# A transformer block pair in float32 on one core: one-bank PSUM tiles for the projections, and combinations recorded ahead of splits

## Chip, cores and metric

The kernel runs on 1 core of a Trainium2 chip. The metric is the device time of one execution in microseconds (us). Before the change three runs gave 1897.74, 1902.15 and 1903.02 us; the median is 1902.15.

## What is computed

Two blocks over 512 tokens of width 2048, all in float32. The first puts 16 learned tokens ahead (528 rows), normalises, projects to queries, keys, values and gates of two attention kinds (8 heads with 2 key/value heads and axial rope; 8 heads of differential attention with a distance bias), gates the results and projects back. The second has stick-breaking attention and a gated linear recurrence. Cut to the part that matters here:

```
hn = rmsnorm(h, pre_norm_g)                      # h: 528 x 2048
proj = einsum('bld,dc->blc', hn, w_in)           # the input projection
qa, ka, va, ga, qb, kb, vb, gb = split(proj)     # ga, gb: gates; qb, kb, vb: differential attention
ya = gqa_axial_mixer(qa, ka, va, ...) * silu(ga)
yb = diff_attn_mixer(qb, kb, vb, ...) * silu(gb)
y  = concatenate([ya, yb]) @ w_out
h  = h + rmsnorm(y, post_norm_g)                 # then the second block on 512 rows
```

## The kernel before

Every float32 operand is split into a high and a low half (`split`, L162: ScalarE casts the high half, L163, and VectorE subtracts it from the source, L164), and a product is three matmul passes over the halves. In the traces L163 and L164 therefore stand for all splits (of weights into wsp, of attention weights into pt, and so on), and L196 for all matmuls, L199 for all transposes.

The work is recorded by a main generator (`main_work`, L1152) and side generators (normalisation, rope, attention heads, the sums of x). `run` (L221) picks the next step by a clock that counts the matmuls' nominal times; a step waits for keys that others post with a delay (`post`, `when`). TensorE's order is fixed by this recording (`_queue`, L187). The order on VectorE, ScalarE and SP is decided afterwards by the recording layer's scheduler, which moves independent instructions past each other. That layer makes an instruction wait for earlier users of the same tile of PSUM.

The order of the main work: keys KA and values VA in channel-major form, queries QA in token-major form (`tm`, L482), the second value (`value(1)`), then 20 pairs of 128-column blocks by a scheme with seven products in place of eight (`seven`, L423), then the output projection O1 and the second block.

In `seven`, TensorE writes four accumulators r[0] to r[3] of one PSUM bank each. A full product is 18 matmuls (6 tiles of 128 rows, three passes); a `rest` adds the 4 remaining tiles, 12 matmuls. The order for a pair is: product 1 into bank 0, product 4 into bank 2, product 5 and rest 6 into bank 0, product 3 into bank 1, rest 6 into bank 3, product 2 into bank 0, product 7 into bank 1, rest 8 into banks 2 and 1, product 9 into bank 3. Between them VectorE combines: L459 reads bank 1 and L460 bank 2 after product 3; L465 and L466 read bank 0 after product 2. Three evacuations end the pair's outputs: `evac_a1` reads bank 0 after rest 6 (L1217 for gates, L1254 for queries and keys, L1280 for values), `evac_b` reads banks 1 and 2 after the rests of 8 (L1222 and L1223 for gates), `evac_a2` reads bank 3 after product 9 (L1230, L1263). p1s keeps product 1 (a ScalarE copy, L450).

The banks come from the pool psj: two tiles of two banks each (L118, L128). Banks 0 and 1 are the halves of one tile, banks 2 and 3 those of the other (L1197).

`produce(p, i)` (L351) splits the weights of product i of pair p and issues the loads and adding transfers that their slots allow. `side_x` (L622) builds the sums and differences of the two halves of x: for six steps j it loads two tiles of x, scales them on ScalarE (L629), combines them on VectorE (L630 to L633) and splits them into x23 and x1s; a last step splits a fourth combination into big once the second value has read that part (key "x2k1"). It begins at 95,000 ns of the recording clock. The first pair waits for all of it (L1196). The tiles of x come from a ring of six (`et`) that attention uses too.

Of the kernel before, what the change touches and what calls it, by code (L numbers as in the profile page):

```python
# [9 lines left out]
F32 = mybir.dt.float32  # L10
# [101 lines left out]
def hybrid_two_block_kernel(ctx: ExitStack, tc: tile.TileContext, wp, wq, wc, xT, xtok, par, lvec, cst, rg, pg, lruw, out):  # L112
# [43 lines left out]
    def halves(ap):  # L156
        return ap.rearrange("p (a b) -> p a b", a=2)
# [60 lines left out]
    def when(*keys):  # L218
        return keys
# [183 lines left out]
    def fm_two(units, ps, lag):  # L403

        w = [None, None]
        for i in range(KT + lag):
            for u, kt in ((0, i), (1, i - lag)):
                if 0 <= kt < KT:
                    if kt % 8 == 0:
                        w[u] = take(units[u], kt // 8, AHEAD - 1)  # L410
                    for pi, (ws, xs) in enumerate(PASSES):
                        for c in range(2):
                            mm(ps[u][:, c, :HL], w[u][:, ws, (kt % 8) * P : (kt % 8 + 1) * P],
                               big[:, xs, kt, c * HL : (c + 1) * HL], kt == 0 and pi == 0, kt == KT - 1 and pi == 2)
                        yield
            if i == KT - 1:
                act.copy(halves(kvraw[0]), ps[0][:, :, :HL])
                post(("kv", 0), 1000)

    def fm_all(unit, ps, after_kt=None):  # L420
        return fm(unit, [(ps[:, 0, :HL], (0, HL)), (ps[:, 1, :HL], (HL, L))], after_kt)

    def seven(p, r, c0a, c0b, evac_a1, evac_b, evac_a2, after=None):  # L423

# [35 lines left out]
        dve.tensor_tensor(us[:], r[2][:, :HL], wv[:], ALU.add)  # L460
# [5 lines left out]
        dve.tensor_tensor(ts[:], r[0][:, :HL], us[:], ALU.add)  # L466
# [12 lines left out]
    def fm_real(unit, ps, x0):  # L479
        return fm(unit, [(ps[:, 0, :], (x0, x0 + NTOK))])  # L480
# [139 lines left out]
    gins = [0]  # L620

    def side_x():  # L622
        ready[("start", 9)] = 95000.0
        yield when(("start", 9), ("kr", 0), ("kr", 1))
        for j in range(KS):
            a, b = et(), et()
            for t, kt in ((a, j), (b, KS + j)):
                nc.sync.dma_start(t, xT[kt])
                act.mul(t, t, g1[:, kt : kt + 1])  # L629
            dve.tensor_tensor(b[:, HL:], a[:, HL:], b[:, HL:], ALU.subtract)  # L630
# [12 lines left out]
    def rope(x, rn, n, c, s, t1, u):  # L643

# [505 lines left out]


    def main_work():  # L1152
        ps = [pjt(), pjt()]
        yield from fm_two((("KA", 0), ("KA", 1)), ps, 3)
        act.copy(halves(kvraw[1]), ps[1][:, :, :HL])
        post(("kv", 1), 1000)
        def value(i, after_kt=None):
            ps = pjt()
            yield from fm_all(("VA", i), ps, after_kt)
            if i:  # L1160
                kvraw[3] = et()
            act.copy(halves(kvraw[2 + i]), ps[:, :, :HL])
            post(("kv", 2 + i), 1000)

        yield from value(0)
# [183 lines left out]
        for hf in range(2):  # L1349
            yield when(("x2", hf))  # L1350
            hc = slice(hf * 256, (hf + 1) * 256)
            for b4 in range(2):
                ps = pjt()
                aps = []
                for i in range(4):
                    ap = ps[:, i // 2, (i % 2) * 256 : (i % 2) * 256 + 256]
                    yield from fm(("XL", 4 * b4 + i), [(ap, (hf * 256, (hf + 1) * 256))])
                    aps.append(ap)
                yield when(("r2", hf))
                for i in range(4):  # L1360
                    b = 4 * b4 + i
                    dve.tensor_tensor(ybuf[:, b, hc], aps[i], rb2[:, hc], ALU.mult)
                    if hf:
                        post(("xl", b))
        for b in range(8):
            ps = pjt()
            yield from fm_real(("GL", b), ps, 0)
            silu2(ps[:, 0, :], rb2, ybuf[:, 8 + b, :])
            post(("gl", b))
        for h in range(8):  # L1370
            ps = pjt()
            yield from fm_real(("GS", h), ps, 0)
            yield when(("xlused", h))
            ins = silu2(ps[:, 0, :], rb2, ybuf[:, h, :])
        with tc.issue_after(ins):
            lnload[1] = act.preload_act_table_set("natural_log_exp_and_others").ins

# [193 lines left out]
```

## Time and profile before

| | |
|---|---|
| median of three runs | 1902.15 us |
| profiled execution | 1903.71 us, span 1901.9 us |
| mean granted TensorE clock | 0.967 |
| busy: TensorE, weight loads, VectorE, ScalarE, GpSimd | 92%, 81%, 60%, 47%, 7% of the span |
| matmuls and transposes | 10288 |
| moved by DMA | 231.72 MB, mean 122 GB/s |
| largest group | 512-column matmuls into pj, 740.0 us |

A row of the busy table gives a stretch, its length, and for each engine its busy time and instruction count; overlapping instructions of one engine count once. A row of the waits names the engine that waited, the tile it wrote and its line, then the engine, tile and line of the instruction that ended the wait, the total in us, the number of waits and the longest. In a timeline row stand the start, the duration, the engine, line, operation, tiles, shape, count, and in brackets the idle time before it with what ended it. A releaser is inferred from semaphore events, so where several conditions were awaited, it is the one that came last.

### The profile page before, as it was taken

How to read it: one execution, taken by the hardware profiler on the slowest of the kernel's cores; microseconds unless marked ns; L12 is line 12 of the kernel's file. 1: busy time of each engine (PE TensorE's matmuls, PEld its weight loads, DVE VectorE, ACT ScalarE, POOL GpSimd, SP SyncE). 2: the span in 40 equal slices, each digit the busy share in tenths (PEclk: the TensorE clock that was granted, in tenths of full speed). 3: DMA queues.
4: the chain of work that ended last, by engine and by line, in shares of the span. 5: the costliest groups of instructions: out<-in, count | busy, mean ns of one | idle time of the engine just before them, and what ended most of it. 6: DMA issues, size and time to landing. Idle time of an engine off the chain costs nothing.

```text
span 1901.9 us, 26572 instructions
## 1 busy us (share of the span) xinstructions
PE 1740.8 (92%) x10288; PEld 1543.1 (81%) x10288; DVE 1139.2 (60%) x1947; ACT 902.5 (47%) x1485; POOL 136.6 (7%) x145
## 2 busy tenths in 40 slices
PE   8997887788887879787998999999999999999998
PEld 8787877788887778787877899988888888888887
DVE  4675666656566668766654676884322375566533
ACT  6354444454444446546643554774222366365411
POOL 0011011100001111110000000010000000000000
PEclk9999989899999899989998999999999999999999
DMA  8335544444544334444334676523232322342223
GB/s 301 116 126 131 158 97 98 110 111 112 138 105 101 88 93 109 97 95 122 128 109 162 220 256 189 158 86 100 89 100 89 100 69 76 100 155 78 89 79 132
DMA packets 82670, 231.72 MB, mean 122 GB/s; under 512 B 9312, under 2 KB 15072, under 8 KB 80864
## 3 DMA queue, kind: packets, MB, share of 16 engines
q1 hardware_dynamic: 73904, 206.43, 33.7%
q0 software_dynamic: 8640, 23.60, 7.9%
q8 instruction: 81, 1.33, 0.3%
q14 instruction: 45, 0.37, 0.1%
HBM read 212.17 MB, written 17.83 MB: 121 GB/s over the span
## 4 chain that ended last, share of the span: by engine, by line
PE 52%; DVE 1%; issue 0%; ACT 0%; DMA 0%; DVEq 0%; ACTq 0%; SPq 0%
PE pj L196 47%; PE pmt L196 1%; PE pss L196 1%; PE bank L196 1%; PE ptt L199 1%; PE pmt L199 0%; PE pss L199 0%; DMA yd<-xmisc 0%; DMA e<-yd 0%; DVE big L164 0%; ACT wsp L163 0%; DVE wsp L164 0%; DVE e L164 0%; DVE e L898 0%; ACT e L901 0%
## 5 line engine op out<-in xcount | busy, mean ns | idle before, releaser
L196 PE MATMUL pj<-wsp,big 128*128 128x512 f32 x3072 | 740.0, 398 | 13.6 <-ACT big L163 8.7
L196 PE MATMUL pj<-big,wsp 128*128 128x264 f32 (+3 forms) x4320 | 662.3, 312 | 86.6 <-DVE xmisc L466 37.1
L196 PEld LDWEIGHTS pj<-big,wsp 128*128 128x128 f32 x4320 | 603.4, 196 | 132.6 <-DVE xmisc L460 35.1
L196 PEld LDWEIGHTS pj<-wsp,big 128*128 128x128 f32 x3072 | 573.1, 189 | 143.0 <-ACT big L163 9.3
L164 DVE TENSOR_TENSOR wsp<-wraw,wsp 128x1024 fp32r<-128x1024 f32 (+3 forms) x399 | 426.4, 1070 | 408.3 <-ACT wsp L163 400.6
L163 ACT CAST wsp<-wraw 128x1024 fp32r<-128x1024 f32 (+3 forms) x399 | 367.9, 924 | 554.0 <-PE pj L196 467.4
L196 PE MATMUL pj<-x,wsp 128*128 128x264 f32 x720 | 112.8, 308 | 40.8 <-DVE e L1217 15.5
L196 PEld LDWEIGHTS pj<-x,wsp 128*128 128x128 f32 x720 | 102.6, 208 | 44.6 <-issue 31.1
L349 POOL DMA_DIRECT2D wraw<-in_wq x60 | 52.8, 880 | 531.0 <-DVE wsp L164 224.2
L164 DVE TENSOR_TENSOR pt<-ptt,pt 128x512 fp32r<-128x512 f32 (+2 forms) x96 | 59.6, 621 | 42.7 <-ACT pt L163 41.8
L163 ACT CAST pt<-ptt 128x512 fp32r<-128x512 f32 (+2 forms) x96 | 50.3, 524 | 67.5 <-PE ptt L199 67.1
L196 PE MATMUL pss<-kk,qq 128*128 128x264 f32 x448 | 75.8, 299 | 3.2 <-DVE sm L898 3.2
L901 ACT ACTIVATE e<-e,sm 128x528 f32<-128x528 f32 x64 | 47.2, 738 | 62.5 <-DVE sm L898 61.9
L196 PE MATMUL pmt<-pt,vv 128*128 128x256 f32 (+1 forms) x528 | 70.2, 281 | 2.9 <-DVE ptail L702 2.9
L196 PEld LDWEIGHTS pmt<-pt,vv 128*128 128x128 f32 x528 | 68.1, 191 | 5.1 <-issue 3.4
L196 PEld LDWEIGHTS pss<-kk,qq 128*128 128x128 f32 x448 | 65.6, 200 | 5.4 <-DVE sm L898 3.7
L898 DVE CUSTOM_DVE_ANT_0 e<-pss,ar 128x528 f32<-128x528 f32 x64 | 45.0, 704 | 25.5 <-PE pss L196 25.3
L199 PE MATMUL ptt<-ident,e 128*128 128x128 f32 x336 | 53.8, 278 | 0.0
L196 PE MATMUL pj<-x1s,wsp 128*128 128x264 f32 x360 | 53.7, 297 | 0.0
L196 PEld LDWEIGHTS pj<-x1s,wsp 128*128 128x128 f32 x360 | 49.6, 201 | 0.2
L1106 POOL TENSOR_SCALAR_AFFINE_SELECT e<-e 128x128 f32<-128x128 f32 x32 | 12.8, 400 | 478.7 <-ACT e L1105 478.7
L199 PEld LDWEIGHTS ptt<-ident,e 128*128 128x128 f32 x336 | 41.0, 143 | 3.5
(251 smaller groups left out, 1417.2 us busy)
## 6 DMA issues: line engine op xcount, KB each, us to landing
wraw<-in_wp SPq DMA_DIRECT2D x215, 512.0 KB, 3.5
wraw<-in_wq SPq DMA_DIRECT2D x80, 384.0 KB, 3.2
wraw<-in_wq POOLq DMA_DIRECT2D x60, 384.0 KB, 4.9
wraw<-in_wc SPq DMA_DIRECT2D x40, 256.0 KB, 2.7
e<-in_xT SPq DMA_DIRECT2D x28, 264.0 KB, 3.9
early<-in_xtok SPq DMA_DIRECT2D x4, 1024.0 KB, 7.4
gated<-e SPq DMA_DIRECT2D x16, 256.0 KB, 2.2
e<-yd SPq DMA_DIRECT2D x16, 256.0 KB, 3.6
```

The source lines that it names most:

```text
L163: act.copy(hi, src)
L164: dve.tensor_tensor(lo, src, f(hi), ALU.subtract)
L196: _queue(nc.tensor.matmul(out, lhsT, rhs, start=start, stop=stop).ins, cost)
L199: _queue(nc.tensor.transpose(out, in_, identity).ins, 110.0)
L349: pool.dma_start(pair_raw[(p, r)], wq[p, q], accum_op=ALU.add)
L898: dve.tensor_tensor_reduce(out=halves(x), in0=s[:, :, :HL], in1=halves(bias[:, b0 : b0 + L]), scale=1.0, scalar=3e38, op0=ALU.add, op1=ALU ...
L901: act.activation(x, x, AF.Exp, scale=-1.0, bias=nm, accum_out=l[:, m : m + 1])
L1106: pool.affine_select(z[:, t * P : w], z[:, t * P : w], [[-1, P]], ALU.is_gt, -1e30, base=0, channel_multiplier=1)
```

## The change

It does four things. (a) The pool psj has four tiles of one bank; the accumulators, and those of `tm` and the other projections, are tiles of their own (a two-part `evac2` copies keys and values out of two of them). (b) In `seven` the combinations and evacuations are recorded ahead of the `produce` that stood before them. (c) `side_x` loses its start at 95,000 ns, so that it begins when both keys have been normalised, fetches the x tiles of step j + 1 before it works on step j, and posts its steps with 4,000 in place of 5,000 ns. (d) The first pair waits only for the six steps; the fourth combination is awaited ahead of product 7.

```
-    psj = ctx.enter_context(tc.tile_pool(name="psj", bufs=2, space=bass.MemoryType.PSUM))
+    psj = ctx.enter_context(tc.tile_pool(name="psj", bufs=4, space=bass.MemoryType.PSUM))
...
     def pjt():
-        return psj.tile([P, 2, 512], F32, tag="pj", name="pj")
+        return psj.tile([P, 512], F32, tag="pj", name="pj")
+
+    def evac2(dst, ps):
+
+        for c in range(2):
+            act.copy(dst[:, c * HL : (c + 1) * HL], ps[c][:, :HL])
...
         yield from product(1, 0, lambda xs, j: big[:, xs, j, X1], allc, True, True)
+        act.copy(p1s[:], r[0][:, :HL])
         produce(p, 6)
-        act.copy(p1s[:], r[0][:, :HL])
...
         yield from product(3, 1, lambda xs, j: x23[:, xs, j, X1], allc, True, True)
-        produce(p, 7)
         dve.tensor_tensor(wv[:], r[1][:, :HL], p1s[:], ALU.subtract)
         dve.tensor_tensor(us[:], r[2][:, :HL], wv[:], ALU.add)
+        produce(p, 7)
         yield from rest(6, 3, 0, False, True, False)
         produce(p + 1, 1)
         yield from product(2, 0, lambda xs, j: x1s[:, xs, j, :], allc, True, True)
-        produce(p, 9)
         dve.tensor_tensor(wv[:], r[0][:, :HL], wv[:], ALU.add)
         dve.tensor_tensor(ts[:], r[0][:, :HL], us[:], ALU.add)
+        produce(p, 9)
+        if p == 0:
+            yield when("x4")
         yield from product(7, 1, lambda xs, j: big[:, xs, j, HL + c0b : L], slice(c0b, HL), True, False)
...
         yield from rest(8, 1, c0b, True, False, True)
+        yield from evac_b()
         produce(p + 1, 4)
-        yield from evac_b()
         yield from product(9, 3, lambda xs, j: big[:, xs, KS + j, X2], allc, False, True)
+        yield from evac_a2()
         produce(p + 1, 5)
-        yield from evac_a2()
...
-        tiles = {p: pjt() for p in sorted({t // 2 for t in toks})}
-        accs = {t: tiles[t // 2][:, t % 2, :] for t in toks}
+        accs = {t: pjt() for t in toks}
...
     def side_x():
-        ready[("start", 9)] = 95000.0
-        yield when(("start", 9), ("kr", 0), ("kr", 1))
+        yield when(("kr", 0), ("kr", 1))
+
+        def fetch(j):
+            x = et(), et()
+            for t, kt in zip(x, (j, KS + j)):
+                nc.sync.dma_start(t, xT[kt])
+            return x
+
+        a, b = fetch(0)
         for j in range(KS):
-            a, b = et(), et()
+            later = fetch(j + 1) if j + 1 < KS else None
             for t, kt in ((a, j), (b, KS + j)):
-                nc.sync.dma_start(t, xT[kt])
                 act.mul(t, t, g1[:, kt : kt + 1])
...
-            post(("xs", j), 5000)
+            post(("xs", j), 4000)
             yield when(("xs", j))
+            if later:
+                a, b = later
...
-        post("x4", 4000)
+        post("x4")
...
-        yield when("xs", "x4")
-        ta, tb = pjt(), pjt()
-        banks = (ta[:, 0], ta[:, 1], tb[:, 0], tb[:, 1])
+        yield when("xs")
+        banks = [pjt() for _ in range(4)]
```

The lines of the changed kernel are 4 to 14 higher. L163, L164, L196 and L199 become L168, L169, L201 and L204; the combinations L459, L460, L465 and L466 become L463, L464, L469 and L470; L822 becomes L836, L826 becomes L840, L368 becomes L373.

TensorE keeps its order but for five transposes at the first pair. What changes there is what it waits for. TensorE in the second pair, from the end of product 3 (x is x23, then big with the rest of product 6, x1s with product 2, big with product 7), before:

```order
L196 MATMUL pj<-x_1057,wsp 128x264 x3
L196 MATMUL pj<-big,wsp 128x264 [waits DVE_49]
L196 MATMUL pj<-big,wsp 128x264 x11
L196 MATMUL pj<-x1s,wsp 128x264 x12
L199 MATMUL pmt<-ident,ar 128x128 [waits PE_49]
L199 MATMUL pmt<-ident,ar 128x128 x3
L196 MATMUL pj<-x1s,wsp 128x264 x6
L196 MATMUL pj<-big,wsp 128x248 [waits DVE_49,Activation_49]
L196 MATMUL pj<-big,wsp 128x248 x2
```

The same place after:

```order
L201 MATMUL pj<-x_835,wsp 128x264 x3
L201 MATMUL pj<-big,wsp 128x264 x12
L201 MATMUL pj<-x1s,wsp 128x264 [waits DVE_49]
L201 MATMUL pj<-x1s,wsp 128x264 x11
L204 MATMUL pmt<-ident,ar 128x128 [waits DVE_49]
L204 MATMUL pmt<-ident,ar 128x128 x3
L201 MATMUL pj<-x1s,wsp 128x264 x6
L201 MATMUL pj<-big,wsp 128x248 [waits DVE_49,Activation_49]
L201 MATMUL pj<-big,wsp 128x248
L201 MATMUL pj<-big,wsp 128x248 [waits DVE_49]
```

The rest of product 6 no longer waits for VectorE; product 2 now waits (for the evacuation of bank 0), and product 7 waits for the two halves of its weights and an older reader of bank 1, where it waited for the readers of bank 0.

VectorE at the same place (wsp rows are weight splits, the first here that of product 7), before:

```order
L822 TENSOR_REDUCE sm<-pss 128x1
L164 TENSOR_TENSOR wsp<-wraw,wsp 128x768
L459 TENSOR_TENSOR xmisc<-pj,xmisc 128x264
L826 RECIPROCAL sm<-sm 128x1
L460 TENSOR_TENSOR xmisc<-pj,xmisc 128x264
L164 TENSOR_TENSOR wsp<-wraw,wsp 128x768
L368 TENSOR_TENSOR wraw<-wraw 128x768
```

And after:

```order
L836 TENSOR_REDUCE sm<-pss 128x1
L463 TENSOR_TENSOR xmisc<-pj,xmisc 128x264
L169 TENSOR_TENSOR wsp<-wraw,wsp 128x768
L840 RECIPROCAL sm<-sm 128x1
L464 TENSOR_TENSOR xmisc<-pj,xmisc 128x264
L169 TENSOR_TENSOR wsp<-wraw,wsp 128x768
L373 TENSOR_TENSOR wraw<-wraw 128x768
```

The first combination and the split of product 7's weights have changed places; the rest of the row is as it was.

SP's transfers from the projection of the queries to the first pairs (in_xT are the tiles of x, in_wp the projection's weights, in_wq and in_wc those of the pairs, qd the queries put aside), before:

```order
L313 DMA wraw<-in_wp 128x1024 x6
L628 DMA e<-in_xT 128x528 x2
L313 DMA wraw<-in_wp 128x1024 x8
L628 DMA e<-in_xT 128x528 x2
L313 DMA wraw<-in_wp 128x1024
L628 DMA e<-in_xT 128x528 x2
L345 DMA wraw<-in_wq 128x768
L628 DMA e<-in_xT 128x528 x2
L345 DMA wraw<-in_wq 128x768
L1174 DMA qd<-e 128x512 x2
```

And after:

```order
L318 DMA wraw<-in_wp 128x1024 x6
L634 DMA e<-in_xT 128x528 x6
L318 DMA wraw<-in_wp 128x1024 x2
L634 DMA e<-in_xT 128x528
L318 DMA wraw<-in_wp 128x1024
L634 DMA e<-in_xT 128x528 x5
L318 DMA wraw<-in_wp 128x1024 x6
L350 DMA wraw<-in_wq 128x768 x2
L1188 DMA qd<-e 128x512 x3
```

All twelve loads of x now stand within the first half of the projection of the queries, ahead of its last six weight tiles. On ScalarE, at the door of the pairs, the copy of the second value (L1162 before, now two copies by `evac2`) stood behind the last cast of x and the cast of the fourth combination; now the cast of the fourth combination and three weight casts stand ahead of it.

More of the change, by code (lines that the diff above doesn't have):

```diff
@@ L412, in fm_two @@
                         for c in range(2):
-                            mm(ps[u][:, c, :HL], w[u][:, ws, (kt % 8) * P : (kt % 8 + 1) * P],
+                            mm(ps[u][c][:, :HL], w[u][:, ws, (kt % 8) * P : (kt % 8 + 1) * P],
                                big[:, xs, kt, c * HL : (c + 1) * HL], kt == 0 and pi == 0, kt == KT - 1 and pi == 2)
@@ L416, in fm_two @@
             if i == KT - 1:
-                act.copy(halves(kvraw[0]), ps[0][:, :, :HL])
+                evac2(kvraw[0], ps[0])
                 post(("kv", 0), 1000)
     def fm_all(unit, ps, after_kt=None):
-        return fm(unit, [(ps[:, 0, :HL], (0, HL)), (ps[:, 1, :HL], (HL, L))], after_kt)
+        return fm(unit, [(ps[0][:, :HL], (0, HL)), (ps[1][:, :HL], (HL, L))], after_kt)
     def seven(p, r, c0a, c0b, evac_a1, evac_b, evac_a2, after=None):
@@ L472, in seven @@
         yield from rest(8, 1, c0b, True, False, True)
+        yield from evac_b()
         produce(p + 1, 4)
-        yield from evac_b()
         yield from product(9, 3, lambda xs, j: big[:, xs, KS + j, X2], allc, False, True)
+        yield from evac_a2()
         produce(p + 1, 5)
-        yield from evac_a2()
     def fm_real(unit, ps, x0):
-        return fm(unit, [(ps[:, 0, :], (x0, x0 + NTOK))])
+        return fm(unit, [(ps, (x0, x0 + NTOK))])
     def tm(units, x0, evac, kgs=range(4), toks=range(NT), before_unit=None, after_unit=None, chore=None):
-        tiles = {p: pjt() for p in sorted({t // 2 for t in toks})}
-        accs = {t: tiles[t // 2][:, t % 2, :] for t in toks}
+        accs = {t: pjt() for t in toks}
         for i, unit in enumerate(units):
@@ L1152, in main_work @@
     def main_work():
-        ps = [pjt(), pjt()]
+        ps = [[pjt(), pjt()] for _ in range(2)]
         yield from fm_two((("KA", 0), ("KA", 1)), ps, 3)
-        act.copy(halves(kvraw[1]), ps[1][:, :, :HL])
+        evac2(kvraw[1], ps[1])
         post(("kv", 1), 1000)
         def value(i, after_kt=None):
-            ps = pjt()
+            ps = [pjt(), pjt()]
             yield from fm_all(("VA", i), ps, after_kt)
@@ L1161, in value @@
                 kvraw[3] = et()
-            act.copy(halves(kvraw[2 + i]), ps[:, :, :HL])
+            evac2(kvraw[2 + i], ps)
             post(("kv", 2 + i), 1000)
@@ L1352, in main_work @@
             for b4 in range(2):
-                ps = pjt()
+                ps = [pjt(), pjt()]
                 aps = []
                 for i in range(4):
-                    ap = ps[:, i // 2, (i % 2) * 256 : (i % 2) * 256 + 256]
+                    ap = ps[i // 2][:, (i % 2) * 256 : (i % 2) * 256 + 256]
                     yield from fm(("XL", 4 * b4 + i), [(ap, (hf * 256, (hf + 1) * 256))])
@@ L1367, in main_work @@
             yield from fm_real(("GL", b), ps, 0)
-            silu2(ps[:, 0, :], rb2, ybuf[:, 8 + b, :])
+            silu2(ps, rb2, ybuf[:, 8 + b, :])
             post(("gl", b))
@@ L1373, in main_work @@
             yield when(("xlused", h))
-            ins = silu2(ps[:, 0, :], rb2, ybuf[:, h, :])
+            ins = silu2(ps, rb2, ybuf[:, h, :])
         with tc.issue_after(ins):
```

## The prediction

> **What bounds the kernel now.** I read the page's first part, then the busy time by stage, then who waited for whom inside the one stage that stands out, then the stretch of rows around two of its waits. First line and stages (each row: stretch, its length, then busy time and instruction count of TensorE, its weight loads, VectorE, ScalarE and GpSimd, then the granted TensorE clock, the DMA share and GB/s):
>
> ```profile
> PE 1740.8 (92%) x10288; PEld 1543.1 (81%) x10288; DVE 1139.2 (60%) x1947; ACT 902.5 (47%) x1485; POOL 136.6 (7%) x145
> 47.20:157.20 110.00, 109.14 (x546) 90.81 (x544) 73.22 (x170) 48.50 (x73) 13.55 (x12) 1.00 0.42 133
> 157.20:163.60 6.40, 0.05 (x1) 0.00 (x0) 4.91 (x9) 5.16 (x7) 0.00 (x0) 0.90 0.46 95
> 163.60:904.00 740.40, 609.39 (x4578) 592.56 (x4579) 485.30 (x920) 363.57 (x669) 89.06 (x82) 0.93 0.44 109
> 904.00:1901.90 997.90, 982.46 (x4879) 821.83 (x4878) 552.14 (x805) 454.90 (x694) 33.19 (x44) 0.99 0.38 122
> ```
>
> TensorE is busy 92% of the span, and the 8% that it lacks lie in one place. Before 157 us and after 904 us it is full (109.1 of 110.0 us, 982.5 of 997.9). Between them, in the 20 pairs of the seven-product scheme, it is idle 740.4 - 609.4 = 131.0 us, at a clock of 0.93 where its neighbours have 1.00 and 0.99, and 6.4 us more are lost at the stage's door. No other engine is full there: VectorE has 485.3 us, 66%. So TensorE sets the pace, and its waits in this stage are what a change can win. Who ended them, 163.5 to 904 us (total, times, longest):
>
> ```profile
> PE pj L196 <- DVE xmisc L466: 37.1, 16, 4.1
> PE pj L196 <- DVE xmisc L460: 30.5, 20, 3.6
> PE pj L196 <- DVE e L1217: 15.5, 7, 6.1
> PE pj L196 <- DVE ar L1254: 9.4, 6, 2.3
> PE pj L196 <- DVE ar L1280: 7.8, 4, 3.8
> ...
> PE pj L196 <- DVE wsp L164: 4.9, 1, 4.9
> PE pj L196 <- DVE sm L174: 4.8, 1, 4.8
> PE pj L196 <- ACT wsp L163: 4.3, 3, 1.5
> PE pj L196 <- DVE e L1223: 3.5, 3, 2.5
> ...
> PE pj L196 <- DVE sm L171: 3.1, 1, 3.1
> ...
> PE pj L196 <- DVE ar L1263: 2.8, 1, 2.8
> ```
>
> L460 and L466 are the second combination after products 3 and 2; L1217, L1254 and L1280 are the evacuations after product 5; L1223 and L1263 belong to the other two evacuations. None of them touches the bank that the waiting matmul writes. L460 reads bank 2, and the 12 matmuls that wait for it write bank 3; L466 and its forerunner read bank 0, and product 7 writes bank 1; L1217 reads bank 0, and product 3 writes bank 1. They are the other bank of the same two-bank tile. (L174 and L171 are tiny steps of a reciprocal root that happened to run as such an evacuation finished.) Together: 37.1 + 30.5 + 15.5 + 9.4 + 7.8 + 4.8 + 3.5 + 3.1 + 2.8 = **114.5 us of 131.0** are waits for a neighbour bank. 16.5 us are others.
>
> **The clock that the waits cost.** I took the 22 stretches at half clock in this stage; first, one in the middle, last and sum, then the matmuls that the middle one follows:
>
> ```profile
> 216.97:220.39 3.42, 3.42 (x19) 3.42 (x18) 2.69 (x7) 0.79 (x2) 1.86 (x2) 0.50 0.39 128
> ...
> 496.87:500.28 3.41, 3.41 (x18) 3.41 (x17) 0.00 (x0) 0.68 (x1) 0.00 (x0) 0.50 0.85 195
> ...
> 875.75:879.16 3.41, 2.93 (x14) 2.62 (x13) 0.43 (x1) 0.62 (x1) 0.00 (x0) 0.50 0.23 45
> sum 99.01, PE 88.65 PEld 86.69 DVE 35.85 ACT 24.39 POOL 6.76; mean PE 4.03 PEld 3.94 DVE 1.63 ACT 1.11 POOL 0.31
> ```
> ```profile
> 496.08 11.30 PE L196 MATMUL pj<-big,wsp 128*128 128x264 f32 x78 [2.26 <-DVE xmisc L466]
> ```
>
> 441 matmuls took 88.65 us in those stretches; the other 4137 of the stage took 609.39 - 88.65 = 520.7 us, 0.126 us each. At that rate the 441 take 55.6, so the half clock costs 33 us, and it comes right behind the waits. [...]
>
> **The change, part by part.** *Four one-bank tiles.* Every wait of the sum above goes at its place; the orders of the program show the wait gone from the rest of product 6 and from product 3 (bar their weights). What is next: product 2, which does write bank 0, now waits for the evacuation after product 5, but 18 + 12 matmuls later (30 x 0.126 = 3.8 us, more with attention work between). Product 7 waits for its weight halves. At most 114.5 + 33 = 147.5 us can come back: a stage of 593 us. VectorE's 485.3 us would then be 82% of it, and in its densest stretch it cannot follow:
>
> ```profile
> 680.00:740.00 60.00, 48.05 (x359) 46.42 (x359) 44.04 (x84) 33.15 (x64) 8.03 (x7) 0.94 0.39 103
> ```
>
> 359 x 0.126 = 45.2 us of TensorE against 44.0 of VectorE. So part of the gain turns into waits for attention work on VectorE. How much, I work out at the second pair, where the rope of a query head falls into the pair (start, duration):
>
> ```profile
> 204.72 0.52 PE L196 MATMUL pj<-x,wsp 128*128 128x264 f32 x3
> ...
> 208.20 1.72 PE L196 MATMUL pj<-big,wsp 128*128 128x264 f32 x12 [2.96 <-DVE xmisc L460]
> ...
> 211.69 0.96 DVE L368 TENSOR_TENSOR wraw<-wraw 128x768 f32<-128x768 f32 x1
> ...
> 215.68 0.59 PE L196 MATMUL pj<-big,wsp 128*128 128x248 f32 x3 [3.13 <-DVE sm L171]
> ...
> 222.58 0.69 DVE L164 TENSOR_TENSOR pt<-ptt,pt 128x512 fp32r<-128x512 f32 x1 [0.63 <-ACT pt L163]
> ...
> 226.05 0.60 PE L199 MATMUL ptt<-ident,e 128*128 128x128 f32 x4
> ```
>
> Product 3 ends at 205.24. From 208.20 to the start of the next wait (215.68 - 3.13 = 212.55) are 4.35 us of work, so product 7 could begin at 205.24 + 4.35 = 209.59. From 215.68 to the transposes at 226.05 are 10.37 us, of which the half clock at 216.97 costs 3.42 - 19 x 0.126 = 1.0; without it TensorE is there at 218.9. These transposes need the split that ends at 223.27. VectorE's row from 211.69 to there is nearly closed (rope of the head, two splits, a reduction) and starts with work on a cast that itself follows the rest of product 6, so it moves up by the 2.96 us of the first wait, to 220.3. TensorE waits 1.4 us. Of 2.96 + 3.13 + 1.0 = 7.1 us, a fifth is passed on. In stretches as dense as 680 to 740 it must be more, in the gates' sparser ones less; I take **a quarter**. Bounds: nothing passed on (593 us), or a stage in which VectorE is never denser than 44.04/60 = 73%, its densest row (485.3/0.734 = 661 us). Gain: 0.75 x 147.5 = **110.6 us**.
>
> *Combinations ahead of splits.* VectorE's count and work stay; the order shows the first combination and the split of product 7 changing places, 0.43 against 0.95 us. The combination fits beside the ScalarE cast that the split needs. Cost 0; cover gone, 0.43 us of the 3.8 us before product 7. After product 8 the first adds of an evacuation go ahead of product 4's split (0.42 + 0.42 us), which is needed 36 matmuls, 4.5 us, later. Cost 0, unless VectorE is late (the slower rival).
>
> *The sums of x earlier; the wait for the fourth moved to product 7.* At the door ScalarE copied the value product only after the last tiles of x, and the transposes at 163.63 waited for the copy:
>
> ```profile
> 153.04 0.74 ACT L629 ACTIVATE e<-e,prm 128x528 f32<-128x528 f32 x1 [1.67 <-DMA e<-in_xT]
> 162.99 0.59 ACT L1162 COPY e<-pj 128x528 f32<-128x528 f32 x1
> 163.63 1.33 PE L199 MATMUL pss<-ident,e 128*128 128x128 f32 x5 [6.39 <-ACT e L1162]
> ```
>
> Now those casts stand some 60 us earlier, and the transposes 12 matmuls into the first product. I take 6 of the 6.4 us as won (bounds 4 and 6.4: three weight casts still stand ahead of the copy). The work goes where TensorE is full and VectorE has 73.2 of 110 us. There one wait exists that it can lengthen: the keys' transposes.
>
> ```profile
> 85.40 0.79 PE L199 MATMUL pss<-ident,early 128*128 128x128 f32 x5 [0.74 <-PE pj L196]
> 126.87 0.43 DVE L630 TENSOR_TENSOR e<-e 128x264 f32<-128x264 f32 x1
> ```
>
> Seven steps of about 0.43 us stand ahead of the second key's rope now: 0 to 3 us, I take 1.5. The twelve loads of x leave SP before the weights of the projection and wait for free tiles; those weights are issued two tiles ahead (2 x 24 matmuls of the 512-column kind), so I cost that at 0, at most a few us. The two copies in place of one for each key and value cost nothing beside full TensorE work.
>
> *After 904 us* the order and the work stay; the four-bank sets free their banks one by one, where TensorE already has 982.5 of 997.9 us: 0, at best 1 or 2.
>
> **Sum.** -110.6 - 6 + 1.5 = -115.1 us. The profiled execution took 1903.71 us in all (its span 1901.9), so 1788.6; the median of the runs lies 1.56 us under it: **1787 us**.
>
> **Rivals.** (1) *VectorE becomes the bound.* It is never denser than 73% in the old trace, and its idle time stays: stage 661, gain 79.2, total 1903.7 - 79.2 - 6 + 1.5 = 1820, median **1818**. For it: 44 against 45 us in the densest row. Against it: much of its idle time is spent on casts that wait for TensorE in turn, so they come sooner when TensorE does:
>
> ```profile
> DVE wsp L164 <- ACT wsp L163: 108.6, 64, 5.2
> ACT wsp L163 <- PE pj L196: 150.7, 76, 6.9
> ```
>
> (2) *Nothing is passed on*: -147.5 - 6.4, median **1748**. Against it the 1.4 us worked out above. [...] (4) *The wait only changes its name*: product 7's weight halves stand behind the combinations on VectorE, and TensorE waits as long for them: 1903.7 - 6 + 1.5, median **1898**. Against it: the halves stand ahead of the second pair of combinations. (5) *Slower*: with evacuations ahead of product 4's split, VectorE is late with it in every pair. It decides from a lag above 4.5 us; at the longest wait on record, 6.1 us, 20 x 6.13 = 122.6 us replace the 114.5, each longer than a half-clock window and so 1 us more, while the old 33 stay: +8.1 + 20 - 6 + 1.5, median **1926**. Against it: the split moves by less than 1 us.
>
> **Chances.** Forecast (1765 to 1807) 0.48; rival 1 0.22; rival 2 0.15; rival 3 0.03; something between rival 1 and no change, 1840 to 1896, 0.04; rival 4 0.04; rival 5 0.04. A measurement of this kernel can tell about 0.3% (6 us) from no change. Faster 0.92, same 0.04, slower 0.04. The range takes in rival 1 and reaches down to rival 2: 1745 to 1838.
>
> **What would show it.** Right: between the door and the stage's end the rows L460 and L466 (by their new lines) and the evacuations after product 5 vanish from TensorE's waits; the stage shrinks from 747 to about 630 us, its clock rises towards 0.98, VectorE's share to about 77%; remaining waits name splits and attention steps. The door's 6.4 us wait is under 1 us. Rival 1 shows as many waits on pt, ptail or score reductions and VectorE near 73%; rival 4 as 100 us of waits on weight splits; rival 5 as long waits of product 4. A stage that is short but a first 157 us that grew by more than 3 us would prove the step on x wrong; a stage time above 900 us that changes by more than 3 us would prove the last one wrong.

## The result and the profile after

The changed kernel takes **1747.1 us** (median of 4 runs, 1746.39 to 1748.41) against 1902.09 for the kernel before beside it: a ratio of **0.919, 95% interval 0.9174 to 0.9206**. The prediction said 1787 with a range of 1745 to 1838. The sign and the mechanism hold, and the time lies in the range, but 40 us below the value given as likeliest and on that of the second rival ("nothing is passed on", 1748). The profiled execution took 1746.56 us, its span 1744.8, so the accounts below go by a gain of 1903.71 - 1746.56 = 157.15 us.

The first part of the page after:

```profile
PE 1691.8 (97%) x10288; PEld 1504.6 (86%) x10288; DVE 1131.7 (65%) x1947; ACT 899.3 (52%) x1489; POOL 135.8 (8%) x145
```

TensorE went from 92% to 97% of the span. Its busy times by stage (columns as in the first fence of the prediction):

```profile
47.00:157.60 110.60, 109.05 (x547) 90.91 (x545) 76.85 (x178) 52.55 (x80) 11.74 (x12) 1.00 0.42 133
157.60:746.20 588.60, 560.23 (x4579) 553.50 (x4578) 476.49 (x919) 361.60 (x672) 89.85 (x83) 0.99 0.56 138
746.20:1744.80 998.60, 982.34 (x4880) 821.95 (x4878) 554.81 (x806) 454.75 (x694) 33.40 (x44) 0.99 0.38 122
```

Everything lies in the second row. Door and pairs took 6.4 + 740.4 = 746.8 us before and 588.6 now. The first 157 us grew by 0.4 us, the time behind the pairs by 0.7. In the pairs TensorE's idle time fell from 131.0 to 588.6 - 560.2 = 28.4 us, and its busy time, for the same matmuls, from 609.4 to 560.2.

Who ended TensorE's waits in the pairs, 158 to 739 us after (total, times, longest):

```profile
PE ptt L204 <- DVE pt L169: 10.3, 5, 3.0
PE pss L201 <- DVE sm L912: 3.8, 3, 3.1
PE pmt L201 <- DVE ptail L716: 3.2, 3, 1.4
PE pj L201 <- DVE wsp L169: 1.8, 2, 1.7
PE pmt L201 <- DVE qq L169: 1.7, 2, 1.2
PE pj L201 <- ACT xmisc L454: 0.9, 2, 0.5
PE pss L201 <- ACT e L838: 0.5, 2, 0.3
```

No combination and no evacuation stands in the list any more; where 20 waits named L460 and 16 named L466, their successors L464 and L470 name none. Most of what remains belongs to attention; weight splits have 1.8 us and the copy of product 1 (L454) 0.9. The timeline at four places, the keys' transposes, the door, the second pair and the start of the output projection (start, duration, and in brackets the wait):

```profile
85.91 0.79 PE L204 MATMUL pss<-ident,early 128*128 128x128 f32 x5 [1.43 <-issue]
...
158.71 0.71 PE L204 MATMUL pss<-ident,e 128*128 128x128 f32 x5
...
190.05 0.52 PE L201 MATMUL pj<-x,wsp 128*128 128x264 f32 x3
190.41 1.61 PE L201 MATMUL pj<-big,wsp 128*128 128x264 f32 x12
191.86 1.63 PE L201 MATMUL pj<-x1s,wsp 128*128 128x264 f32 x12
...
205.02 0.65 PE L204 MATMUL ptt<-ident,e 128*128 128x128 f32 x4 [1.65 <-DVE pt L169]
...
745.21 1.22 PE L201 MATMUL pj<-wsp,big 128*128 128x512 f32 x2 [6.18 <-DVE wsp L169]
```

The 12 matmuls of the rest of product 6 (190.41) follow product 3 without a gap; before, 2.96 us lay between them. The second transposes of that pair wait 1.65 us for VectorE's split, where the prediction had worked out 1.4. The door's wait of 6.39 us is gone. The output projection waits 6.18 us for its first weights, 4.88 before.

### The profile page after: what moved, and what is told of

Read it like the earlier page. It is cut to its first block, busy times and chain, and to the rows that moved or that the text cites. A ratio compares the mean times of both kernels' runs of the same rounds, so it can differ in the third digit from the quotient of the medians.

```text
span 1744.8 us, 26494 instructions
## 1 busy us (share of the span) xinstructions
PE 1691.8 (97%) x10288; PEld 1504.6 (86%) x10288; DVE 1131.7 (65%) x1947; ACT 899.3 (52%) x1489; POOL 135.8 (8%) x145
## 4 chain that ended last, share of the span: by engine, by line
PE 77%; DVE 4%; DMA 1%; ACT 1%; issue 1%; POOL 0%; SPq 0%; ACTq 0%; DVEq 0%; POOLq 0%
PE pj L201 67%; PE pmt L201 3%; PE pss L201 3%; PE ptt L204 2%; PE bank L201 1%; DVE wsp L169 1%; PE pmt L204 1%; PE pss L204 1%; DVE e L912 0%; DMA wraw<-in_wc 0%; DMA yd<-xmisc 0%; DVE ar L960 0%; ACT wsp L168 0%; DVE pt L169 0%; DMA wraw<-in_wp 0%
## 5 line engine op out<-in xcount | busy, mean ns | idle before, releaser
L201 PE MATMUL pj<-wsp,big 128*128 128x512 f32 x3072 | 739.4, 397 | 16.5 <-ACT big L168 10.4
L201 PEld LDWEIGHTS pj<-wsp,big 128*128 128x128 f32 x3072 | 572.7, 189 | 145.5 <-ACT big L168 10.8
L201 PE MATMUL pj<-big,wsp 128*128 128x264 f32 (+3 forms) x4320 | 636.7, 304 | 9.3 <-ACT big L543 5.6
L201 PEld LDWEIGHTS pj<-big,wsp 128*128 128x128 f32 x4320 | 582.8, 189 | 46.4 <-ACT big L543 5.9
L169 DVE TENSOR_TENSOR wsp<-wraw,wsp 128x1024 fp32r<-128x1024 f32 (+3 forms) x399 | 425.0, 1068 | 300.5 <-ACT wsp L168 294.9
L168 ACT CAST wsp<-wraw 128x1024 fp32r<-128x1024 f32 (+3 forms) x399 | 366.4, 922 | 412.9 <-PE pj L201 330.2
L201 PE MATMUL pj<-x,wsp 128*128 128x264 f32 x720 | 102.1, 288 | 0.2 <-DVE wsp L169 0.2
L201 PEld LDWEIGHTS pj<-x,wsp 128*128 128x128 f32 x720 | 93.6, 190 | 0.6 <-DVE wsp L169 0.4
L169 DVE TENSOR_TENSOR pt<-ptt,pt 128x512 fp32r<-128x512 f32 (+2 forms) x96 | 59.5, 619 | 30.8 <-ACT pt L168 29.5
L201 PE MATMUL pss<-kk,qq 128*128 128x264 f32 x448 | 73.7, 293 | 4.3 <-DVE sm L912 3.8
L201 PE MATMUL pmt<-pt,vv 128*128 128x256 f32 (+1 forms) x528 | 72.4, 287 | 4.9 <-DVE ptail L716 3.2
L201 PEld LDWEIGHTS pmt<-pt,vv 128*128 128x128 f32 x528 | 69.7, 196 | 7.8 <-issue 3.3
L168 ACT CAST pt<-ptt 128x512 fp32r<-128x512 f32 (+2 forms) x96 | 50.2, 523 | 40.8 <-PE ptt L204 40.5
L201 PEld LDWEIGHTS pss<-kk,qq 128*128 128x128 f32 x448 | 63.4, 193 | 7.3 <-DVE sm L912 4.6
L204 PE MATMUL ptt<-ident,e 128*128 128x128 f32 x336 | 53.2, 275 | 10.3 <-DVE pt L169 10.3
L204 PEld LDWEIGHTS ptt<-ident,e 128*128 128x128 f32 x336 | 40.0, 141 | 14.7 <-DVE pt L169 8.6
L201 PE MATMUL pj<-x1s,wsp 128*128 128x264 f32 x360 | 50.8, 287 | 0.0
L838 ACT ACTIVATE e<-pss,sm 128x528 f32<-128x528 f32 x32 | 22.5, 702 | 48.3 <-DVE sm L836 48.2
```

The lines of the kernel that those rows point to most:

```text
L168: act.copy(hi, src)
L169: dve.tensor_tensor(lo, src, f(hi), ALU.subtract)
L201: _queue(nc.tensor.matmul(out, lhsT, rhs, start=start, stop=stop).ins, cost)
L204: _queue(nc.tensor.transpose(out, in_, identity).ins, 110.0)
L838: act.activation(halves(x), sv, AF.Exp, bias=nm, accum_out=l[:, 0:1])
```

## The experiments

Each ratio is to the kernel before, run on the same chip; it had medians of 1901.82, 1903.7 and 1902.81 us in the three sets. Differences in us are between medians. Where a run is compared with the changed kernel's 1747.1 us, the two come from different sets, and a difference of 2 us can be that of the sets.

### Which part of the change does it

*Banks alone*: only part (a), one-bank tiles, in the kernel before.

```
-    psj = ctx.enter_context(tc.tile_pool(name="psj", bufs=2, space=bass.MemoryType.PSUM))
+    psj = ctx.enter_context(tc.tile_pool(name="psj", bufs=4, space=bass.MemoryType.PSUM))
-        ta, tb = pjt(), pjt()
-        banks = (ta[:, 0], ta[:, 1], tb[:, 0], tb[:, 1])
+        banks = [pjt() for _ in range(4)]
...
```

> Part (a) alone: four one-bank tiles; combinations stay behind the splits, x and the door as before. Theory 1 (the waits were for the neighbour bank, and nothing else of the change matters in the pairs): the waits of L460 and L466 vanish, the time is that of the changed kernel plus the door's 6.4 us and a little clock: 1753 to 1760 us. Rival (the order of combinations and splits carries a good part): VectorE is late with combinations and splits, and waits of 1 us or more remain in most pairs: 1775 us or more.

Measured: 1758.79 us, 0.9252 (0.9226 to 0.9279). Part (a) alone gives 143 of the 155 us. Two of its waits that the full change does not have, or has smaller:

```profile
PE pss L204 <- ACT e L134: 5.3, 1, 5.3
PE pj L201 <- ACT xmisc L455: 4.1, 7, 2.0
```

The first is the door (the copy of the second value), the second the copy of product 1 behind the weight casts: what (c), (d) and (b) take away.

*Order alone*: only part (b), the combinations and evacuations recorded ahead of `produce`, on two-bank tiles.

```
         yield from product(3, 1, lambda xs, j: x23[:, xs, j, X1], allc, True, True)
-        produce(p, 7)
         dve.tensor_tensor(wv[:], r[1][:, :HL], p1s[:], ALU.subtract)
         dve.tensor_tensor(us[:], r[2][:, :HL], wv[:], ALU.add)
+        produce(p, 7)
...
```

> Part (b) alone: combinations and evacuations ahead of the splits, two-bank tiles as before. Theory 1: TensorE still waits for the same reads of the neighbour bank, which come at most one split (0.95 us) earlier at two places of 20 pairs: 0 to 38 us less, 1864 to 1902 us, with L460 and L466 still the longest waits. Rival (order carries a good part): 1850 us or less.

Measured: 1869.83 us, 0.9841 (0.9818 to 0.9864). TensorE's waits, 163 to 870 us (L459 and L465 are the second combinations here):

```profile
PE pj L196 <- DVE xmisc L459: 30.5, 20, 3.5
PE pj L196 <- DVE xmisc L465: 22.5, 15, 2.9
PE pj L196 <- DVE e L1217: 15.9, 7, 6.4
PE pj L196 <- DVE ar L1254: 9.3, 6, 2.1
```

The order shortens the waits for the second pair of combinations from 37.1 to 22.5 us and leaves the others much as they were. As long as the false wait stands, the earlier combinations are worth 32 us: some 15 of these waits, and some 15 of TensorE's busy time (1740.8 us before, 1725.6 here). Once it is gone, they are worth nothing that can be told:

*After without the order*: the changed kernel with part (b) undone.

```
         yield from product(3, 1, lambda xs, j: x23[:, xs, j, X1], allc, True, True)
+        produce(p, 7)
         dve.tensor_tensor(wv[:], r[1][:, :HL], p1s[:], ALU.subtract)
         dve.tensor_tensor(us[:], r[2][:, :HL], wv[:], ALU.add)
-        produce(p, 7)
...
```

> The changed kernel without part (b): splits recorded ahead of combinations again. Theory 1 (only the banks and the door count): within 0.3% of the changed kernel, 1742 to 1752 us. Rival (order matters once the banks are free, since VectorE is 81% full): 1760 us or more, with waits on weight splits or attention splits.

Measured: 1753.54 us, 0.9201 (0.9178 to 0.9224), an interval that overlaps that of the changed kernel and a median just above the expected stretch. Its trace has waits of 4.4 us for the copy of product 1, which part (b) also moves, where the changed kernel has 0.9. So nothing speaks against the cost of 0 that the prediction gave the order, within a few us.

*x alone* and *after without x*: only parts (c) and (d), and all but these.

```
-        ready[("start", 9)] = 95000.0
-        yield when(("start", 9), ("kr", 0), ("kr", 1))
+        yield when(("kr", 0), ("kr", 1))
...
-        yield when("xs", "x4")
+        yield when("xs")
...
```

> Parts (c) and (d) alone: sums of x early, first pair not held for the fourth. Theory: the door's wait of 6.4 us shrinks to under 1 us and its half clock goes: 1893 to 1897 us. Rival (the x work only moves the cost into the projection of the queries): within 3 us of 1902.

> The changed kernel without parts (c) and (d). Theory: the door's wait is back (6 us and some half clock), 1753 to 1758 us. Rival (the early x work delays the projection of the queries by as much as it wins): 1745 to 1749 us.

Measured: 1894.66 us, 0.9958 (0.9936 to 0.9981; 10 runs), and 1754.75 us, 0.9211 (0.9189 to 0.9232). The door is worth 7 us in the first comparison. In the second it is 8 us by the medians and 4 by the ratios, and the two intervals overlap; the door's wait is in the trace of the run without (c) and (d) (5.2 us) and not in that of the changed kernel.

### Are they really waits for a neighbour bank?

*Paired 0-3 and 1-2*: the kernel before with one line changed. Which banks share a tile is swapped; the tiles stay two banks wide, and no other line moves.

```
-        banks = (ta[:, 0], ta[:, 1], tb[:, 0], tb[:, 1])
+        banks = (ta[:, 0], tb[:, 0], tb[:, 1], ta[:, 1])
```

> The kernel before with one line changed: accumulators 0 and 3 share one two-bank tile and 1 and 2 the other, in place of 0 and 1, and 2 and 3. Pool, order and x as before. Theory 1: what counts is who is whose neighbour. Now the reads of a neighbour come 18 matmuls or more ahead of the write, but for the evacuation after product 9 (bank 3), which product 1 of the next pair (bank 0) follows at once. 20 such waits of 1 to 3 us stay of the 114.5 us: 1780 to 1815 us, and the waits of L460 and L466 vanish. Rival (the one-bank pool helps by something else than neighbours, such as its four buffers): no change, 1895 to 1905 us.

Measured: 1813.44 us, 0.9547 (0.9522 to 0.9572). TensorE's waits, 163 to 810 us:

```profile
PE pj L196 <- DVE e L1230: 19.6, 8, 4.9
PE pj L196 <- DVE ar L1263: 15.3, 7, 5.8
PE pj L196 <- DVE ar L1289: 9.8, 4, 3.2
```

The waits for L460 and L466 are gone, and new ones stand where bank 0 now has a neighbour that is read late: the three lines of `evac_a2` read bank 3, and product 1 of the next pair, which writes bank 0, waits 44.7 us for them. TensorE runs the same 10288 instructions in the same order; on VectorE and ScalarE the scheduler moved some (about a hundred of VectorE's 1947). That does not explain why the old waits vanish in every pair and new ones stand just at the new partner. So the wait follows the tile and not the bank. Together with *banks alone*, where no such wait is left, this settles the cause.

### Why almost nothing was passed on

*Load 4* and *load 8*: the changed kernel with 4 or 8 VectorE reductions per pair (80, 160 in all) that nobody reads, at the four places of the combinations and splits.

```
+    def more():
+        dve.tensor_reduce(idle, f(big[:, 0, 15, :512]), axis=AX.X, op=ALU.max)
```

> The changed kernel with extra VectorE work: behind four of the nine splits of a pair a reduction over 128x512 that nothing uses, about 0.69 us each, 80 in all, 55 us. VectorE goes from 469 to about 524 us of a stage of 581, 90%. Theory 2 (TensorE sets the pace and VectorE's place in the queue has slack): less than a third shows, 1750 to 1765 us. Rival (VectorE is at its limit above the 73% that it reached before): all of it shows, 1795 us or more.

> As load_4 with two reductions at each of the four places: 160 in all, 110 us; VectorE would need 579 of 581 us. Theory 2: now VectorE is the bound, since its waits cannot all be filled: 1785 to 1830 us. Rival (VectorE at its limit already): 1850 us or more.

Measured: 1755.82 us, 0.9211 (0.9186 to 0.9236), and 1786.39 us, 0.9378 (0.9353 to 0.9402). Neither tests what it was meant to. The reductions depend on nothing in a pair, and the scheduler put them where it liked: the 80 of load 4 all ended by 151 us, ahead of the pairs. That both times lie in the expected stretch confirms nothing. Of load 8, VectorE's time in the reductions alone (stretch, length, busy time and count):

```profile
158.00:200.00 42.00, 25.27 (x37) 0.88 0.46 106
200.00:250.00 50.00, 26.00 (x39) 0.83 0.39 97
250.00:782.00 532.00, 0.00 (x0) 0.98 0.55 134
```

And all engines in the second of these stretches:

```profile
200.00:250.00 50.00, 35.10 (x239) 33.68 (x239) 49.03 (x91) 16.99 (x28) 5.35 (x6) 0.83 0.39 97
```

The other 84 ran ahead of the pairs. All that these two runs say is that where VectorE is really full, 49.03 of 50 us, TensorE gets 35.10; of its waits from 158 to 782 us, 43.3 of 44.5 us name VectorE.

*Pinned 2, 4, 8*: so the reductions were tied to their place by their operands, which exist only between two combinations of one pair; 1, 2 and 4 of them at each of two places, 40, 80 and 160 in all (the code is that of the 40).

```
         dve.tensor_tensor(us[:], r[2][:, :HL], wv[:], ALU.add)
+        more(1, 1)
...
         dve.tensor_tensor(ts[:], r[0][:, :HL], us[:], ALU.add)
+        more(2, 1)
...
+    def more(i, n):
+        for _ in range(n):
+            dve.tensor_reduce(idle, operands[1][:, i * HL : (i + 2) * HL], axis=AX.X, op=ALU.max)
```

> The changed kernel with 40 extra VectorE reductions that nobody reads, two in each pair of products: one behind the combination that makes v, which reads u and v, and one behind the combination that makes ts, which reads v and ts. Their operands exist only inside the pair, so they cannot move ahead of the pairs as the free reductions of the two runs before did. In those runs a 128x512 reduction took 0.68 us, so 40 make about 28 us, and VectorE's busy time in the stretch 158 to 739 would be about 498 us of 581. Theory (VectorE has slack in the pairs, which is why nothing was passed on): 1747 to 1753 us. Rival (VectorE's chain decides in the pairs, each us of it is passed on): about 1775 us.

> As the run with 40 pinned reductions, with 80: two behind each of the two combinations, about 56 us, VectorE's busy time in the pairs about 526 us. Theory (slack of 581 less 470, 111 us, uneven): 1750 to 1770 us, with the loss showing first as waits of the split transposes for VectorE's pt split. Rival (passed on): about 1803 us.

> As the run with 40 pinned reductions, with 160: four behind each of the two combinations, about 112 us, which would fill VectorE in the pairs (about 582 us of 581). Theory (slack): the slack is used up here and only here, 1785 to 1840 us, with TensorE waiting for VectorE in most pairs. Rival (passed on in full): about 1859 us.

| reductions | added on VectorE | median | ratio (interval) | over 1747.1 | passed on |
|---|---|---|---|---|---|
| 40 | 27.8 us | 1749.18 | 0.9183 (0.9164 to 0.9202) | 2.1 | 8% |
| 80 | 55.7 | 1763.35 | 0.9262 (0.9245 to 0.9279) | 16.3 | 29% |
| 160 | 111.4 | 1801.79 | 0.9462 (0.9446 to 0.9478) | 54.7 | 49% |

By the ratios in place of the medians, the three cost -1, 14 and 52 us. So the first 28 us cost nothing that can be told from no change, the next 28 some 14, the last 56 some 38: the slack runs out gradually, and not "here and only here" at 160, as had been expected. All three medians lie where the theory had them; the rival (every us is passed on) was 26 to 57 us too high. With 160, the stage and the waits that fill it:

```profile
157.60:793.00 635.40, 580.03 (x4581) 565.72 (x4579) 559.02 (x1066) 354.13 (x662) 89.12 (x83) 0.97 0.52 125
```
```profile
PE pj L201 <- DVE wsp L169: 13.2, 10, 6.6
PE ptt L204 <- DVE pt L169: 9.9, 8, 3.0
PE pss L201 <- DVE sm L919: 9.3, 6, 4.4
PE pmt L201 <- DVE ptail L723: 8.5, 5, 2.3
```

VectorE at 88% still leaves TensorE 580 of 635 us. Of the 13.2 us, 6.6 are the one wait at the start of the output projection, which was there without the load too (6.18). In the pairs the waits that grew are those for weight splits (1.8 us without load, 6.6 here), score reductions (3.8, 9.3) and tails (3.2, 8.5), not first those for the pt splits, as had been expected: these were 11.6 us with 80, 9.9 with 160 and 10.3 with none.

### The wait that remains

*Early first weights*: the changed kernel with the output projection's first weight tile loaded and cast within the last pair. The tile lands where product 9 of that pair still reads its own weights, so that one product multiplies other numbers; its matmuls are as many and as long.

```
             def after():
                 for kt in range(KS):
                     split_ready(kt)
+                for _ in load_next():
+                    pass
```

> The changed kernel with one step moved: the first weight tile of the output projection is loaded and cast during the last pair of the products, not behind it. The TensorE order stays. Theory (the wait of 6.18 us for the cast of the first weight tile at 745.21 us is that tile's arrival and nothing else): the wait shrinks to 1 to 2 us, 1740 to 1744 us. Rival (the tile waits for a slot that the last product holds, or its cast pushes the casts of y aside): within 3 us of 1747.

Measured: 1743.81 us, 0.9156 (0.9138 to 0.9174). Around the last pair's end:

```profile
741.55 0.64 PE L201 MATMUL pj<-big,wsp 128*128 128x264 f32 x3 [1.54 <-DVE wsp L169]
742.02 0.65 PE L201 MATMUL pss<-kk,qq 128*128 128x264 f32 x4
742.51 1.99 PE L201 MATMUL pj<-big,wsp 128*128 128x264 f32 x15
744.34 1.09 PE L201 MATMUL pj<-wsp,big 128*128 128x512 f32 x4
```

The wait of 6.18 us is gone, and product 9 waits 1.54 us for VectorE's half of the split in its place: 4.6 us by the trace, 3.3 by the medians, and the intervals of the ratios only touch. The wait is thus one for that tile. Not all of it is the tile's arrival: in the trace of the changed kernel its cast ends at 742.18 us and VectorE, busy with other work, begins its half at 743.94, so some 1.8 us are VectorE's order. A kernel that may use this needs a slot that product 9 does not hold; that was not tried, and how much of the lateness is the slot's stays open.

## Why the prediction was right, and 40 us too high

**What bounds the kernel: right.** TensorE's waits in the pairs were what there was to win, and 114.5 us of them were for a neighbour bank. The swap of partners shows that they follow the tile, and with one-bank tiles all of them are gone.

**Passed on, a quarter: wrong, and some 22 of the 40 us.** "I take a quarter" was spread over both terms, 0.75 x 147.5 = 110.6 us. In place of the 114.5 us, the other idle time of the pairs rose from 131.0 - 114.5 = 16.5 to 28.4 us: 11.9 us, **a tenth**, were passed on (1.3 of them the longer wait of the output projection). The example was good (1.4 us worked out, 1.65 measured), but it was one of five places:

```profile
249.08 1.12 PE L204 MATMUL ptt<-ident,e 128*128 128x128 f32 x4 [2.96 <-DVE pt L169]
...
297.87 0.65 PE L204 MATMUL ptt<-ident,e 128*128 128x128 f32 x4 [3.00 <-DVE pt L169]
```

All five waits for pt end before 300 us, in the first quarter of the pairs, and I had taken the second pair for the mean of 20. "In stretches as dense as 680 to 740 it must be more" is not borne out either. The same work of TensorE, counted along its order, and below it a stretch in which VectorE is denser still, after:

```profile
561.34:610.38 49.04, 45.38 (x360) 44.55 (x359) 42.62 (x86) 32.99 (x63) 8.25 (x6) 0.97 0.46 115
...
606.00:656.00 50.00, 50.00 (x417) 49.82 (x416) 44.69 (x86) 34.06 (x64) 8.61 (x7) 1.00 0.55 133
```

In the first, TensorE is idle 3.7 us, where it was idle 12.0 us in 680 to 740 before, 1.7 of them for attention already: 2 us came anew for some 10 that went, a fifth, as in the second pair and not more. In the second, VectorE is busy 89% and TensorE has not one gap. VectorE's share before was no measure of what it could do, since much of its idle time was the echo of TensorE's. After, in the pairs:

```profile
DVE wsp L169 <- ACT wsp L168: 33.5, 45, 2.5
ACT wsp L168 <- PE pj L201: 43.1, 46, 3.9
```

These two were 108.6 and 150.7 us. ScalarE waited for TensorE to free a slot, and VectorE for ScalarE's cast; when TensorE's waits went, so did 75 us of VectorE's. The prediction held this row against its first rival and yet did not use it against its own quarter. The pinned reductions bear it out: VectorE had room for 28 us more work in the pairs at no cost that can be told.

**The clock, 33 us: right in kind and size, but not the whole.** The half-clock stretches in the pairs after, and their sum:

```profile
248.83:252.24 3.41, 3.16 (x15) 3.01 (x16) 1.81 (x5) 2.50 (x7) 0.00 (x0) 0.50 0.79 250
573.10:576.51 3.41, 3.19 (x15) 3.22 (x16) 1.62 (x4) 2.15 (x6) 0.00 (x0) 0.50 0.22 87
661.84:668.67 6.83, 5.41 (x25) 5.13 (x25) 4.04 (x9) 5.37 (x13) 0.00 (x0) 0.50 0.40 125
sum 13.65, PE 11.76 PEld 11.36 DVE 7.47 ACT 10.02 POOL 0.00; mean PE 3.92 PEld 3.79 DVE 2.49 ACT 3.34 POOL 0.00
```

The other 4579 - 55 matmuls took (560.23 - 11.76) / 4524 = 0.121 us each. At that rate the old stretches cost 88.65 - 441 x 0.121 = 35.3 us and the new ones 5.1, so 30 us came back where 0.75 x 33 = 24.7 had been counted.

Busy time fell by 49.2 us in all, though, and the other **19 us** were in no term: this is the rest of the 40. Some 2 of them are clock again. The 22 stretches of the prediction leave out a first one at half clock, 162.36 to 169.19 us, behind the door's wait; its 26 matmuls and transposes from 163.60 on took 5.55 us, 2.4 more than at 0.121. Matmuls at full clock had taken 0.126 us, and I took this for their price. Part of it was the price of the waits. Three rows of before, around two of them:

```profile
489.93 1.72 PE L196 MATMUL pj<-big,wsp 128*128 128x264 f32 x12 [0.99 <-DVE xmisc L460]
491.49 2.34 PE L196 MATMUL pj<-x1s,wsp 128*128 128x264 f32 x18
496.08 2.34 PE L196 MATMUL pj<-big,wsp 128*128 128x264 f32 x12 [2.26 <-DVE xmisc L466]
```

Behind a wait, 12 matmuls take 491.49 - 489.93 = 1.56 us to the next ones; without one, 191.86 - 190.41 = 1.45. Ahead of a wait the 18 end after 2.34 us, where 18 x 0.121 = 2.18. That makes 0.11 + 0.16 = 0.27 us per wait in which TensorE counts as busy without a matmul more done. The other waits of both traces agree. Away from waits and half clock, a matmul or transpose took 0.120 us from start to start in both kernels; the first one behind a wait took 0.09 us more (mean of 64 places before, 16 after), and the last one ahead of a wait counts as busy 0.16 us longer (65 and 19). The profile's ends of matmuls are modelled, so the 0.16 is rough. TensorE had 69 waits in the pairs before and has 20 now, each time with that of the output projection: an estimate of 49 x 0.27 = 13 us. The other 4 stay unexplained.

**The sum, mended.** Against the gain forecast in the pairs of 110.6 us, idle time gave 131.0 - 28.4 = 102.6 where 0.75 x 114.5 = 85.9 was taken (+16.7), and busy time 49.2 where 0.75 x 33 = 24.7 was taken (+24.4). With 1.1 us less lost ahead of the pairs, 0.4 us more won at the door and 0.7 us lost behind the pairs, that is 41.9 us, against the 42.0 between the 1788.6 forecast for the profiled execution and the 1746.56 that it took.

**The smaller steps.** *Order*: 0 forecast, nothing that can be told measured. *Door*: 6 of 6.4 us forecast, 6.4 by the trace, some 7 by the medians of *x alone*. *x ahead of the pairs*: +1.5 at the keys' transposes forecast; that wait grew from 0.74 to 1.43 us. *After 904 us*: 0 forecast, +0.7 measured. *What would show it*: a stage of 588.6 us for the 630 named, a clock of 0.99 for 0.98, VectorE at 476.5 of 588.6, 81%, for 77%.

**The rivals.** The first (VectorE never denser than 73%) falls by the row at 89%; nor was 680 to 740 the densest stretch of before, since 672 to 732 us has VectorE busy 45.88 us, 76%. The second had the time, 1748, and partly by chance: it set 0 where 11.9 us were passed on, and lacked the 19 us of busy time that were in no term. The fourth and fifth fall by the list of waits, in which weight splits have 1.8 us in two waits. The 1 us of half clock that the fifth adds per wait was an estimate from the stretch at 216.97; before, six of the seven waits of TensorE longer than 3.41 us in the pairs have half clock within or behind them, the one of 3.56 us that ends at 699.92 has not.

## What to carry to other kernels

Look in a list of waits for a matmul into one bank that waits for a reader of another. If the two share a tile, the wait can be an artefact of how dependencies are tracked. Here it was one: one-bank tiles alone won 143 of the 155 us, the partner decided how much it cost (1902 us, or 1813 with the partners swapped), and a change of partner is a one-line test. A wait of TensorE cost its length here, by estimate some 0.3 us around it that count as busy, and, in 22 stretches behind such waits, half clock (35.3 us in all). VectorE's 66% next to a waiting TensorE said little about its limit (81% after, 89% in one stretch): follow an engine's own waits, and if they lead back to TensorE, as VectorE's did here, expect them to shrink with it (108.6 to 33.5 us here).

## What the runs showed of the hardware

**Half clock came behind windows with up to 1.52 us of work.** In the trace of before, each window of 3.413 us on one grid from 152 to 900 us is at full or at half clock as a whole, and the stretches at half clock start a whole number of windows apart (216.97 and 496.87: 82). The windows that half clock follows are those in which TensorE was least busy, with an overlap around 1.5 us. Five windows of before on that grid (third column TensorE's busy time, third from the end the clock):

```profile
281.83:285.24 3.41, 1.49 (x14) 1.29 (x12) 1.24 (x4) 2.40 (x5) 0.89 (x1) 1.00 0.36 33
285.24:288.66 3.42, 0.58 (x5) 0.61 (x6) 3.15 (x13) 0.64 (x2) 0.00 (x0) 1.00 0.80 197
288.66:292.07 3.41, 3.41 (x18) 3.41 (x17) 2.71 (x7) 0.05 (x1) 1.81 (x2) 0.50 0.03 7
...
493.46:496.87 3.41, 1.15 (x10) 0.97 (x9) 2.48 (x4) 0.83 (x1) 0.88 (x1) 1.00 0.17 14
496.87:500.28 3.41, 3.41 (x18) 3.41 (x17) 0.00 (x0) 0.68 (x1) 0.00 (x0) 0.50 0.85 195
```

A window with 1.49 us of work is followed by full clock, those with 0.58 and 1.15 by half. Over all windows of before between 152 and 900 us, the 23 at full clock that half clock follows were busy 0 to 1.52 us, and the least busy ones that full clock follows 1.49, 1.51 and 1.56; in the kernel with swapped partners the two kinds overlap between 1.59 and 1.75 us. So in these kernels waits that left TensorE less than about 1.5 us of work in a window were enough; in 493.46:496.87 it was the one wait of 2.26 us, which left 1.15. Of the windows of before at half clock, those busy up to 2.67 us were followed by half clock again and those from 2.93 us on by full clock; of the two between, the one with 2.75 us was followed by full clock and the one with 2.78 by half.

**TensorE was full beside a VectorE at 89%**, in the stretch of 606 to 656 us after (50.00 and 44.69 of 50 us); with VectorE at 98% (load 8, 200 to 250 us, 49.03 of 50) it was busy 70% (35.10).
